# State-space products on whole operands: states copied by eight groups, tables reordered, a block's 48 small matmuls in one bunch

## The chip, the core and the metric

One core of one Trainium2 chip runs the whole program. The metric is device time in microseconds (us) of one execution. The core's engines named here are PE (TensorE: matmuls, and PEld, its weight loads), DVE (VectorE), ACT (ScalarE), POOL (GpSimd) and SP (SyncE, which issues most of the DMAs). Each has its own instruction order and they meet through semaphores.

## The reference, cut to what matters

The model is a first block (attention, mLSTM, mixture of experts) and a second block of two layers; everything here happens in the last layer, `s5_branch`, with one sequence of 256 positions and 128 groups of 16 features with 64 complex states each:

```python
u, z, xq = split_cols(h @ w_in, [SEQ_WIDTH, MIX_WIDTH, XA_WIDTH])      # 2048, 3072, 1024
y = s5_chunked(u in groups, ab, bb, c)   # x_t = ab x_{t-1} + bb u_t ;  y_t = re(c x_t)
y = jax.nn.gelu(y + d * u)
y = y * jax.nn.sigmoid(y @ w_glu + b_glu)
xa = memory_attention(xq, mem_n, w_kv)
x = x + (jnp.concatenate([y, xa], axis=-1) * jax.nn.silu(z)) @ w_out
```

## The kernel before

All weights are fp32. Each is split into a high and a low fp32r part, ACT making the high one (`whi`, L267) and DVE the low one (`wlo`, L268), and a product is three matmuls (`mm3`). A dense product `dense_t` is 48 matmuls of 128x256 on PE; after every 12 of them it lets another generator advance, so that other work is interleaved in PE's order. Every matmul is issued at L280, so the rows are told apart by tile: `ps` is a dense product, `st` a state-space product, `at` the attention, `acc` the output projection.

The state-space part splits the 256 positions into 64 chunks of 4. The 128 groups are worked on in eight blocks `jb`, each of 8 columns j and two halves x of 64 partitions. One state-space product is 64x64 on 64 partitions in fp32 and shows as two matmul rows on PE.

The layer goes through these stages:

1. **Inputs and states.** The input projections `su` give u, which goes through memory (`ud`, written by ACT's queue, L1719) and comes back as `U[jb]` (L1679). `states(jb)` multiplies U by the table `tab1` (tile `tab`, two products per j and x, real and imaginary states) and by `tab3` (tile `wu`, the product inside the chunk). It yields after every second j, and so a block's 48 products lie in PE's order in four passes between the dense products of `su` and `sx`. DVE and ACT then copy the states of every chunk to `Xs` (L1694, L1692), and DVE adds d·u to U (L1696, L1697).
2. **Scan.** `scanned(half)` is the recurrence over chunks in `Xs`, on DVE (L1638 to L1641, four operations a step, 21 steps a half). Half 0 can start after block 3, half 1 after block 7. `scan(n)` puts n steps into the order at fixed places of the stages around it.
3. **Memory attention** (`at`), then twelve `z_block`s (dense products of `sz`, each closed by a multiply on DVE, L1614), with scan steps between them.
4. **Output stage.** For each jb: the table `tab2` (L1603, two buffers, each freed by the product two blocks before) times `Xs` gives `st`; DVE adds U (L1747), ACT makes the Gelu (L1748) and issues a write to memory (`yd`, L1749), SP issues two reads back (`yy`, L1754, four buffers), ACT and DVE split each `yy` (tiles `y`, `U`), POOL multiplies it into `zs` (L1759). Beside this PE runs the output projection of the attention features f = 16 to 23 (`acc`, 24 matmuls each; its operands `gyh` and `gyl` are split from `xa` by ACT and DVE).
5. **Gated output.** For f = 0 to 15 a dense product with `sglu` on all split y (`ps`, 48 matmuls) and then 24 `acc` matmuls, to the end.

Operands are read as they lie: in L1745 the weights are `w[x, j, i::2]` (every second element) and the moving states `Xs[x, i, :, 8 * jb + j]` (every 64th element); in L1688 `wu[x, j]` is every eighth element, while `tab1`'s parts and U lie side by side.

No engine's order is written out by hand for the change: the order follows from the code, buffer waits and a scheduler.

Of the kernel before, what the change touches and what calls it, by code (L numbers as in the profile page):

```python
# [15 lines left out]
AF = mybir.ActivationFunctionType  # L16
# [191 lines left out]
class Kern:  # L208
# [1115 lines left out]
    def s5_out(self, P, jb):  # L1324

        nc, e = self.nc, self.nc.gpsimd
        raw = self.t(P, [128, 2, 8, 16], "s_raw", bufs=2)
        e.dma_start(raw, self.io["sbc"][jb][:, 2:4])
        t2 = self.t(P, [128, 8, 64, 2], "s_t2")
        tmp = self.t(P, [128, 8, 16], "s_tmp")  # L1330
        A = [self.s5ab[:, i, 8 * jb:8 * jb + 8, None].to_broadcast([128, 8, 16]) for i in range(2)]
        e.tensor_scalar(raw[:, 1], raw[:, 1], -1.0, None, op0=OP.mult)
        y = (raw[:, 0], raw[:, 1])
        for k in range(4):
            o = tuple(t2[:, :, 16 * k:16 * k + 16, i] for i in range(2))
            e.tensor_mul(o[0], y[0], A[0])
            e.tensor_mul(tmp, y[1], A[1])
            e.tensor_add(o[0], o[0], tmp)
            e.tensor_mul(o[1], y[1], A[0])
            e.tensor_mul(tmp, y[0], A[1])  # L1340
            e.tensor_sub(o[1], o[1], tmp)
            y = o
        e.dma_start(self.tab2[jb], t2.rearrange("p j s i -> p j (s i)"))

    def s5_steps(self, G, P):

# [241 lines left out]
    def s5(self, out):  # L1588
        nc, io, tc = self.nc, self.io, self.tc
        x3 = self.xT  # L1590
        self.psum_banks(ps=2, st=3, at=3)
        with ExitStack() as S:
            P = S.enter_context(tc.tile_pool(name="s", bufs=1))
            zs = self.t(P, [128, 16, T], "zs")
            xa = self.t(P, [128, 8, T], "xa")

            Xs = self.t(P, [128, 2, 64, 64], "Xs")
            U = []
            halves = [slice(0, 64), slice(64, 128)]

            def table(jb, tab):
                w = self.t(P, [128, 8, 128], "tab", bufs=2)
                nc.sync.dma_start(w, tab[jb].rearrange("p j s -> p j s"))  # L1603
                return w

            with ExitStack() as S2:
# [36 lines left out]
                def scanned(half):  # L1643

                    gs = slice(32 * half, 32 * half + 32)
                    Xb = Xs.rearrange("p i (b s) g -> p i b s g", b=8)[..., gs]
                    for n in range(1, 8):
                        onto(Xb[:, :, :, n], Xb[:, :, :, n - 1], 0, gs, [128, 2, 8, 32])
                        yield
                    for b in range(1, 8):  # L1650
                        onto(Xb[:, :, b, 7:8], Xb[:, :, b - 1, 7:8], 7, gs, [128, 2, 1, 32])
                        yield
                    for b in range(1, 8):
                        onto(Xb[:, :, b, 0:7], Xb[:, :, b - 1, 7:8], slice(0, 7), gs, [128, 2, 7, 32])
                        yield
# [3 lines left out]
                def scan(n):  # L1659
                    for _ in range(n):  # L1660
                        next(steps, None)


                with tc.tile_pool(name="su", bufs=1) as S1:
                    with tc.issue_after(self.mark.ins):
                        d = self.t(S1, [128, 64], "sd")
                        nc.sync.dma_start(d, io["sd"])
                        nc.gpsimd.memset(Xs[:, :, 0], 0.0)
                        self.s5_steps(P, S1)

                    def inputs(jb):
                        return table(jb, self.tab1.rearrange("b p j i s -> b p j (i s)")).rearrange("p j (i s) -> p j i s", i=2)

                    def states(jb, w):
                        wu = self.t(S1, [128, 4, 128], "wu", bufs=2)
                        nc.sync.dma_start(wu, self.tab3[jb])
                        wu = wu.rearrange("p k (h j) -> p j (k h)", j=8)
                        U.append(self.t(P, [128, 8, 64], "U", bufs=8))
                        nc.sync.dma_start(U[jb].rearrange("p j c -> p (j c)"), self.ud[jb])  # L1679
                        ps = [self.psum("st") for _ in range(3)]  # L1680
                        pj = [p.rearrange("p (j c) -> p j c", j=8) for p in ps]
                        for j in range(8):
                            for i in range(3):
                                for x in halves:
                                    self.mm(pj[i][x, j], wu[x, j] if i == 2 else w[x, j, i], U[jb][x, j], True, True)
                            if j % 2:
                                yield
                        for i in range(2):  # L1688
                            src = ps[i].rearrange("p (j c) -> p c j", j=8)[:, 0:63]
                            dst = Xs[:, i, 1:64, 8 * jb:8 * jb + 8]  # L1690
                            if i:
                                nc.scalar.activation(dst, src, AF.Copy)  # L1692
                            else:
                                nc.vector.tensor_copy(dst, src)  # L1694
                        t = self.t(W, [128, 8, 64], "zt")
                        nc.vector.tensor_mul(t, U[jb], d[:, 8 * jb:8 * jb + 8, None].to_broadcast([128, 8, 64]))  # L1696
                        nc.vector.tensor_add(U[jb], t, pj[2])  # L1697

                    def all_states():
                        with tc.issue_after(self.mark.ins):  # L1700
                            w = inputs(0)
                        yield
                        for jb in range(8):
                            with tc.issue_after(self.mark.ins):
                                now, w = w, inputs(jb + 1) if jb < 7 else None
                                yield from states(jb, now)
                            if jb >= 4:
                                scan(SCAN_EARLY)

                    st = all_states()  # L1710
                    next(st)
                    for n in range(4):
                        for b in (n, n + 4):
                            ps = self.dense_t(io["su"][b], h, st if 2 * n + b // 4 >= 3 else iter(())) if b else self.su0
                            u = self.t(W, [128, 2, T], "zt")
                            nc.vector.tensor_mul(u, ps, bc(r, 2))
                            for a in range(2):
                                dst = self.ud[2 * n + a].rearrange("(q s h) (j c) -> q (h j) s c", q=2, s=4, j=8)
                                nc.scalar.dma_start(dst[b // 4], u[:, a].rearrange("p (s c) -> p s c", s=4))  # L1719
                    for b in range(4):  # L1720
                        ps = self.dense_t(io["sx"][b], h, st)
                        nc.vector.tensor_mul(xa[:, 2 * b:2 * b + 2], ps, bc(r, 2))
                    for _ in st:
                        pass
# [4 lines left out]
                for b in (8, 9, 10, 11, 0, 1, 2, 3, 4, 5, 6, 7):  # L1729
                    if b == 6:  # L1730
                        scan(64)
                    z_block(b)
                    scan(SCAN_LATER)

            self.psum_banks(acc=4, ps=2, st=2)
            Y = S.enter_context(tc.tile_pool(name="sg", bufs=1))
# [1 line left out]
            ys = [[None] * 16, [None] * 16]  # L1738
            for jb in range(8):
                w = table(jb, self.tab2)  # L1740
                p = self.psum("st")
                for j in range(8):
                    for i in range(2):
                        for x in halves:
                            self.mm(p[x, 64 * j:64 * j + 64], w[x, j, i::2], Xs[x, i, :, 8 * jb + j], i == 0, i == 1)  # L1745
                y = U[jb].rearrange("p j c -> p (j c)")
                nc.vector.tensor_add(y, p, y)  # L1747
                nc.scalar.activation(y, y, AF.Gelu_apprx_tanh)  # L1748
                nc.scalar.dma_start(self.yd[jb], y)  # L1749
                yv = self.yd[jb].rearrange("(q s h) (j c) -> q (h j) s c", q=2, s=4, j=8)  # L1750
                for par in range(2):
                    f = 8 * par + jb
                    u = self.t(W, [128, T], "yy", bufs=4)
                    nc.sync.dma_start(u.rearrange("p (s c) -> p s c", s=4), yv[par])  # L1754
                    y2 = self.t(P, [128, 2, T], "U", F32R, bufs=8) if par else self.t(Y, [128, 2, T], "y%d" % jb, F32R)
                    for n in range(2):
                        ys[n][f] = y2[:, n]
                    self.split(u, ys[0][f], ys[1][f])
                    nc.gpsimd.tensor_mul(zs[:, f], zs[:, f], u)  # L1759
# [82 lines left out]
```

## Time and profile before

| what | value |
|---|---|
| median of 3 runs | 1498.87 us (1495.82 to 1501.35) |
| the profiled execution's own time | 1499.36 us |
| its span, first to last instruction | 1497.3 us |
| PE busy | 1337.9 us, 89% |
| PEld busy | 1065.1 us, 71% |
| DVE busy | 761.6 us, 51% |
| ACT busy | 549.8 us, 37% |
| POOL busy | 323.3 us, 22% |
| mean granted clock of PE | 0.93 |

The shares are averages over the whole program, and the last layer is only its last 425 us or so. What a stage can gain has to be read from that stage's windows and chain. The profiled execution is 0.5 us above the median. Records of PE start where a matmul starts and their ends are modelled, so that the distance of two starts says what one cost.

### The profile page before, as it was taken

What the parts mean: (1) busy time and instruction counts of PE and PEld (TensorE: products, weight loads), DVE (VectorE), ACT (ScalarE), POOL (GpSimd) and SP (SyncE); (2) the same over time, 40 slices, a digit from 0 to 9 for tenths busy, and PEclk for the clock granted to TensorE, in tenths of its full rate; (3) what the DMA queues carried; (4) which work ended last, traced back from release to release, by engine and by line L of the source; (5) the groups of instructions that cost most, each with busy time, mean ns of one, the idle gap of its engine ahead of it and who ended that gap; (6) DMA issues with size and microseconds to landing.
All of it is one profiled execution on the core that took longest, in us unless ns stands there. A gap on an engine that the chain in (4) does not pass through costs nothing. (4 is left out here: it accounts for less than half of the span.)

```text
span 1497.3 us, 25797 instructions
## 1 busy us (share of the span) xinstructions
PE 1337.9 (89%) x10632; PEld 1065.1 (71%) x10632; DVE 761.6 (51%) x1498; ACT 549.8 (37%) x859; POOL 323.3 (22%) x450
## 2 busy tenths in 40 slices
PE   5999998987887888686679999999999999999997
PEld 2777796553454555341159989999888988999997
DVE  2766454812233321010047686588846899665553
ACT  3754553321211122110034435644522355444443
POOL 0031121412223231200008887111400000030001
PEclk8899999998988999896689999999999999999998
DMA  9776764999999999999994525889766534675540
GB/s 364 277 268 250 268 246 174 379 400 420 420 408 415 420 408 420 420 421 374 421 370 156 204 92 178 259 251 320 265 203 204 170 138 147 213 205 189 178 141 29
DMA packets 87626, 414.86 MB, mean 277 GB/s; under 512 B 26432, under 2 KB 28016, under 8 KB 43472
## 3 DMA queue, kind: packets, MB, share of 16 engines
q1 hardware_dynamic: 66768, 381.85, 66.9%
q0 software_dynamic: 8016, 22.13, 4.7%
q10 hardware_dynamic: 12720, 9.18, 1.9%
q8 instruction: 86, 1.41, 0.4%
q14 instruction: 36, 0.29, 0.1%
HBM read 392.90 MB, written 20.22 MB: 276 GB/s over the span
## 5 line engine op out<-in xcount | busy, mean ns | idle before, releaser
L267 ACT ACTIVATE whi<-w 128x1024 fp32r<-128x1024 f32 x252 | 263.7, 1056 | 329.8 <-PE ps L280 249.9
L268 DVE TENSOR_TENSOR wlo<-w,whi 128x1024 fp32r<-128x1024 f32 x222 | 273.4, 1240 | 145.2 <-ACT whi L267 144.6
L280 PE MATMUL ps<-hh,whi 128*128 128x256 f32 x928 | 272.8, 294 | 11.2 <-DVE zt L1614 5.0
L280 PE MATMUL ps<-hh,wlo 128*128 128x256 f32 x928 | 266.9, 288 | 2.0 <-DVE wlo L268 1.8
L280 PE MATMUL ps<-hl,whi 128*128 128x256 f32 x928 | 267.8, 289 | 0.9 <-DVE hl L1579 0.7
L280 PEld LDWEIGHTS ps<-hh,whi 128*128 128x128 f32 x928 | 179.0, 193 | 19.5 <-issue 9.1
L280 PEld LDWEIGHTS ps<-hh,wlo 128*128 128x128 f32 x928 | 178.8, 193 | 4.5 <-DVE wlo L268 2.6
L280 PEld LDWEIGHTS ps<-hl,whi 128*128 128x128 f32 x928 | 179.0, 193 | 2.0 <-DVE hl L1579 0.7
L280 PE MATMUL A<-w,xg 128*32 128x512 f32 x984 | 139.6, 667 | 33.8 <-DMA w<-in_w 32.9
L280 PE MATMUL acc<-gyl,whi 128*128 128x256 f32 x384 | 109.1, 284 | 0.6 <-DVE gyl L268 0.6
L280 PE MATMUL acc<-gyh,wlo 128*128 128x256 f32 x384 | 109.1, 284 | 0.0
L280 PE MATMUL acc<-gyh,whi 128*128 128x256 f32 x384 | 108.2, 282 | 0.0
L268 POOL TENSOR_TENSOR wlo<-w,whi 128x1024 fp32r<-128x1024 f32 x30 | 70.6, 2368 | 167.1 <-ACT whi L267 166.9
L934 DVE SCALAR_TENSOR_TENSOR xT<-m,mod,xT 128x256 f32<-128x256 f32 x64 | 27.8, 480 | 142.7 <-PE m L280 142.7
L280 PEld LDWEIGHTS A<-w,xg 128*32 128x32 f32 x984 | 23.8, 114 | 102.3 <-DMA w<-in_w 73.2
L280 PE MATMUL A<-w,gT 128*32 128x512 f32 x512 | 75.0, 687 | 24.1 <-DMA w<-in_w 16.5
L960 DVE TENSOR_TENSOR g<-g,A 128x512 f32<-128x512 f32 x8 | 5.5, 687 | 134.3 <-PE A L280 134.3
L280 PEld LDWEIGHTS acc<-gyl,whi 128*128 128x128 f32 x384 | 72.7, 189 | 1.5 <-DVE gyl L268 0.8
L280 PEld LDWEIGHTS acc<-gyh,whi 128*128 128x128 f32 x384 | 73.2, 191 | 0.2 <-issue 0.2
L280 PEld LDWEIGHTS acc<-gyh,wlo 128*128 128x128 f32 x384 | 72.9, 190 | 0.2 <-issue 0.2
L1759 POOL TENSOR_TENSOR zs<-zs,yy 128x256 f32<-128x256 f32 x16 | 14.7, 935 | 236.9 <-DMA yy<-yd 236.1
L280 PE MATMUL ps<-wlo,hh 128*128 128x256 f32 x192 | 56.1, 292 | 3.4 <-DVE wlo L268 3.4
(585 smaller groups left out, 2766.8 us busy)
## 6 DMA issues: line engine op xcount, KB each, us to landing
w<-in_w SPq DMA_DIRECT2D x187, 1024.0 KB, 11.5
w<-in_wada SPq DMA_DIRECT2D x24, 1024.0 KB, 7.3
w<-in_wo SPq DMA_DIRECT2D x24, 1024.0 KB, 5.3
w<-in_sglu SPq DMA_DIRECT2D x16, 1024.0 KB, 4.9
w<-in_gz SPq DMA_DIRECT2D x12, 1024.0 KB, 6.9
w<-in_sz SPq DMA_DIRECT2D x12, 1024.0 KB, 4.8
w<-in_win SPq DMA_DIRECT2D x10, 1024.0 KB, 7.1
w<-in_xk SPq DMA_DIRECT2D x8, 1024.0 KB, 9.7
```

Of the source, the lines that this page charges most:

```text
L267: self.nc.scalar.activation(hi, src, AF.Copy)
L268: (eng or self.nc.vector).tensor_sub(lo, src, hi.bitcast(F32))
L280: self.nc.tensor.matmul(ps, l, r, start=start, stop=stop, **kw)
L934: self.nc.vector.scalar_tensor_tensor(self.xT[:, f], pc[:, T * c:T * c + T], self.m(5)[:, f:f + 1], self.xT[:, f], op0=OP.mult, op1=OP.add)
L960: nc.vector.tensor_mul(g1, g1, p3)
L1759: nc.gpsimd.tensor_mul(zs[:, f], zs[:, f], u)
```

## The change

- `tab2` is stored with the real parts of a j ahead of the imaginary ones (the POOL code that builds it writes them so), and so a weight operand is 64 elements side by side.
- `Xs` becomes two tiles, one for each half of the scan. A new helper `by_group` has ACT copy a block of 8 columns to `Xg`, with the 64 chunks of one column side by side (128x1024, eight copies: one in the attention stage, seven in the output stage, two buffers). The output products read `Xg`.
- `tab3` is loaded to a free part of `zs`, and ACT copies it (128x512, eight copies) to `wu` so that a weight operand is side by side.
- A block's 48 products in `states` are issued in one bunch. The four yields come behind them.

```diff
-        t2 = self.t(P, [128, 8, 64, 2], "s_t2")
+        t2 = self.t(P, [128, 8, 2, 64], "s_t2")
...
-            Xs = self.t(P, [128, 2, 64, 64], "Xs")
+            Xs = [self.t(P, [128, 2, 64, 32], "Xs%d" % n) for n in range(2)]
...
+                def by_group(pool, jb):
+                    Xg.append(self.t(pool, [128, 2, 8, 64], "Xg", bufs=1 if jb == 0 else 2))
+                    nc.scalar.activation(Xg[jb], Xs[jb // 4][:, :, :, 8 * (jb % 4):8 * (jb % 4) + 8].rearrange("p i c j -> p i j c"),
+                                         AF.Copy)
...
-                        wu = self.t(S1, [128, 4, 128], "wu", bufs=2)
-                        nc.sync.dma_start(wu, self.tab3[jb])
-                        wu = wu.rearrange("p k (h j) -> p j (k h)", j=8)
+                        raw = zs[:, 2 * (jb % 4):2 * (jb % 4) + 2].rearrange("p f t -> p (f t)")
+                        nc.sync.dma_start(raw, self.tab3[jb].rearrange("p k c -> p (k c)"))
+                        wu = self.t(S1, [128, 8, 64], "wu", bufs=2)
+                        nc.scalar.activation(wu.rearrange("p j (k h) -> p j k h", k=4),
+                                             raw.rearrange("p (k h j) -> p j k h", k=4, j=8), AF.Copy)
...
                                     self.mm(pj[i][x, j], wu[x, j] if i == 2 else w[x, j, i], U[jb][x, j], True, True)
-                            if j % 2:
-                                yield
...
                         nc.vector.tensor_add(U[jb], t, pj[2])
+                        for _ in range(4):
+                            yield
...
+                by_group(P, 0)
...
                 w = table(jb, self.tab2)
+                if jb < 7:
+                    by_group(Y, jb + 1)
...
-                            self.mm(p[x, 64 * j:64 * j + 64], w[x, j, i::2], Xs[x, i, :, 8 * jb + j], i == 0, i == 1)
+                            self.mm(p[x, 64 * j:64 * j + 64], w[x, j, 64 * i:64 * i + 64], Xg[jb][x, i, j], i == 0, i == 1)
```

On PE, in the input and state stage, a piece of the difference between the two orders (`x4` is four products in a row: the real and the imaginary part of one j on both halves of the partitions):

```order
 L280 MATMUL st<-U,tab 64x64 x4
 L280 MATMUL st<-U,wu 64x64 x2
-L280 MATMUL ps<-hl,whi 128x256
-L280 MATMUL ps<-hh,wlo 128x256
-L280 MATMUL ps<-hh,whi 128x256
-L280 MATMUL ps<-hl,whi 128x256
-L280 MATMUL ps<-hh,wlo 128x256
 L280 MATMUL st<-U,tab 64x64 x4
 L280 MATMUL st<-U,wu 64x64 x2
```

The dense rows between two j are gone from here and stand behind the bunch: before there are 43 separate stretches of `st` rows among the `ps` rows of this stage, now 8 stretches of 48 products. The products (384) and the `ps` rows between the first of them and the first `at` (413) are as many as before.

SP's DMA issues in the same stage, around the loads of blocks 2 and 3, before:

```order
L262 DMA w<-in_sx 128x2048
L1679 DMA U<-ud 128x512 x2
L1603 DMA tab<-tab_84 128x1024
L1676 DMA wu<-tab_86 128x512
L262 DMA w<-in_sx 128x2048
```

and in the changed kernel (L1690 is U's load, L1685 the load of `tab3` to `zs`):

```order
L262 DMA w<-in_sx 128x2048
L1603 DMA tab<-tab_84 128x1024
L1690 DMA U<-ud 128x512 x2
L1685 DMA zs<-tab_86 128x512
L262 DMA w<-in_sx 128x2048
```

The loads U(2) and U(3) moved behind the load of `tab` for block 3, which waits until the bunch of block 1 has let go of its buffer.

ACT in the output stage, before (with the tiles' numbers; `U_11117` is U of block 7, its Gelu is L1748 and its write L1749):

```order
L267 ACTIVATE gyh_12831<-xa_9999 128x256
L267 ACTIVATE whi_12903<-w_12901 128x1024
L1748 ACTIVATE U_11117<-U_11117 128x512
L267 ACTIVATE y5_12585<-yy_12583 128x256
L1749 DMA yd_87<-U_11117 128x512
L267 ACTIVATE U_12591<-yy_12589 128x256
```

and in the changed kernel (`U_11127` is U of block 7, Gelu L1762, write L1763):

```order
L267 ACTIVATE gyh_12857<-xa_9999 128x256
L267 ACTIVATE U_12563<-yy_12561 128x256
L267 ACTIVATE whi_12895<-w_12861 128x1024
L267 ACTIVATE whi_12929<-w_12927 128x1024
L267 ACTIVATE y5_12609<-yy_12607 128x256
L1762 ACTIVATE U_11127<-U_11127 128x512
L267 ACTIVATE U_12615<-yy_12613 128x256
L1763 DMA yd_87<-U_11127 128x512
```

The Gelu of block 7 moved behind the split `y5`, which waits for block 5's read back from memory. In the same stage ACT has the seven copies `Xg` and one load of an activation table more than before; ahead of the Gelu of block 0 stand the copies `Xg` of blocks 1 and 2, the `gyh` of f = 16 and 17 and a table load.

SP's issues in the output stage of the changed kernel (`yy` is L1768):

```order
L262 DMA w<-in_wo 128x2048
L1603 DMA tab<-tab_85 128x1024 x2
L1768 DMA yy<-yd 128x4x64 x2
L1603 DMA tab<-tab_85 128x1024
L1768 DMA yy<-yd 128x4x64 x2
L1603 DMA tab<-tab_85 128x1024 x2
L1768 DMA yy<-yd 128x4x64 x4
L1603 DMA tab<-tab_85 128x1024
```

The table of block 4 is behind the first two `yy`, those of blocks 5 and 6 behind the next two, and that of block 7 behind the `yy` of blocks 2 and 3; before, the tables of blocks 3 and 4 stood together ahead of the first `yy` and the fifth's behind four of them.

## Rows read from the trace of the kernel before

**Rows 1.** Windows of the last layer, one line each. The columns are start:end, length, then for PE, PEld, DVE, ACT and POOL the busy us and the number of instructions, the granted clock, the share of DMA engines busy and GB/s. The first two make up the stage of inputs and states, cut where the scan begins; then attention and z-blocks; the output stage; the gated output.

```profile
1099.78:1145.31 45.53, 45.53 (x582) 40.95 (x582) 19.65 (x25) 10.82 (x12) 0.00 (x0) 1.00 0.62 193
1145.31:1190.00 44.69, 44.69 (x573) 40.72 (x571) 36.78 (x68) 10.56 (x12) 0.00 (x0) 1.00 0.56 184
1190.00:1290.48 100.48, 91.30 (x687) 87.43 (x685) 97.71 (x199) 55.01 (x71) 0.00 (x0) 0.98 0.44 151
1290.48:1344.81 54.33, 53.74 (x706) 51.86 (x707) 30.29 (x42) 24.71 (x45) 14.68 (x16) 0.97 0.73 228
1344.81:1497.30 152.49, 143.73 (x1188) 143.35 (x1187) 72.98 (x90) 64.65 (x88) 7.25 (x8) 0.96 0.38 132
```

**Rows 2.** The chain of work that ended last, input and state stage: start, us, engine, tile, line, matmul rows.

```profile
1101.73 1.09 PE st L280 x24
1102.82 1.62 PE ps L280 x12
...
1187.71 5.89 PE ps L280 x48
1193.60 0.86 PE at L280 x4
```

**Rows 3.** Timeline of PE at two places of that stage: start, us with the modelled end, engine, line, tile and operands, rows.

```profile
1107.07 0.45 PE L280 MATMUL st<-U,tab 64*64 64x64 f32 x8
1107.35 0.40 PE L280 MATMUL st<-U,wu 64*64 64x64 f32 x4
1107.59 0.40 PE L280 MATMUL st<-U,tab 64*64 64x64 f32 x8
1107.82 0.40 PE L280 MATMUL st<-U,wu 64*64 64x64 f32 x4
...
1181.17 0.68 PE L280 MATMUL st<-U,tab 64*64 64x64 f32 x16
1181.78 0.39 PE L280 MATMUL ps<-hl,whi 128*128 128x256 f32 x1
```

**Rows 4.** Tile `st`: matmuls by operand, with the duration of one in ns (minimum/median/maximum) and the first and last start.

```profile
L280 PE MATMUL st<-U,tab x512: 218/218/267, 1099.8 to 1187.3; 64*64 64x64 f32 x171
L280 PE MATMUL st<-Xs,tab x512: 283/285/309, 1290.5 to 1329.6; 64*64 64x64 f32 x171
L280 PE MATMUL st<-U,wu x256: 275/280/330, 1100.0 to 1187.4; 64*64 64x64 f32 x128
```

**Rows 5.** Timeline of DVE at the first scan step and at the last z-block, and between them one weight split from the chain of work that ended last.

```profile
1145.31 0.68 DVE L1638 TENSOR_TENSOR zs<-Xs,pw 128x512 f32<-128x512 f32 x1
...
1271.05 1.14 DVE wlo L268
...
1289.75 0.68 DVE L1614 TENSOR_TENSOR zt<-ps,r 128x512 f32<-128x512 f32 x1
```

**Rows 6.** The chain of work that ended last, output stage and the first gated product (columns as in rows 2; a block's 32 products are 64 rows, and a few records are missing, so that x125 stands for the 128 rows of blocks 0 and 1).

```profile
1290.48 7.33 PE st L280 x125
1299.20 3.72 PE st L280 x64
...
1334.30 2.72 DMA yy<-yd
...
1337.91 0.96 DVE gyl L268
1338.91 5.89 PE acc L280 x47
1344.81 11.52 PE ps L280 x96
```

**Rows 7.** ACT's groups of instructions in the output stage (busy us, mean ns of one, idle before them and what ended it), and from tile `Xs` its copy of the states from PSUM, which writes every 64th element (ns minimum/median/maximum).

```profile
L267 ACT ACTIVATE whi<-w 128x1024 fp32r<-128x1024 f32 x8 | 8.4, 1053 | 6.2 <-PE acc L280 6.2
L1748 ACT ACTIVATE U<-U 128x512 f32<-128x512 f32 x8 | 5.1, 633 | 15.6 <-DVE U L1747 15.6
L267 ACT ACTIVATE y<-yy 128x256 fp32r<-128x256 f32 x8 | 3.3, 407 | 3.4 <-DMA yy<-yd 2.9 <-ACT U L1748 0.4
L1748 ACT ACT_TABLE_LOAD x1 | 1.3, 1283 | 0.0
...
L1692 ACT ACTIVATE Xs<-st x8: 576/592/593, 1109.1 to 1187.5; 128x504 f32<-128x504 f32 x8
```

**Rows 8.** DMAs, us from issue to landing (minimum/median/maximum): tiles `ud`, `U`, `yd`, `yy`, and `tab` in the output stage, in this order; one issue on SP's queue in the output stage; then POOL's multiply of `yy`, from the page's costliest groups.

```profile
DMA to landing us min/median/max: 2.0/4.9/8.3
DMA to landing us min/median/max: 2.3/4.3/6.2
DMA to landing us min/median/max: 2.2/4.2/6.0
DMA to landing us min/median/max: 2.2/4.1/5.6
DMA to landing us min/median/max: 4.1/4.9/5.7
...
1309.35 0.33 SPq L1603 DMA_DIRECT2D tab<-tab  x1
...
L1759 POOL TENSOR_TENSOR zs<-zs,yy 128x256 f32<-128x256 f32 x16 | 14.7, 935 | 236.9 <-DMA yy<-yd 236.1
```

**Rows 9.** A window of dense matmuls of 128x256 a little before the state stage (columns as in rows 1).

```profile
1076.00:1079.30 3.30, 3.30 (x16) 3.30 (x17) 2.38 (x4) 1.58 (x3) 3.22 (x5) 0.50 0.78 276
```

More of the change, by code (lines that the diff above doesn't have):

```diff
@@ L1334, in s5_out @@
         for k in range(4):
-            o = tuple(t2[:, :, 16 * k:16 * k + 16, i] for i in range(2))
+            o = tuple(t2[:, :, i, 16 * k:16 * k + 16] for i in range(2))
             e.tensor_mul(o[0], y[0], A[0])
@@ L1342, in s5_out @@
             y = o
-        e.dma_start(self.tab2[jb], t2.rearrange("p j s i -> p j (s i)"))
+        e.dma_start(self.tab2[jb], t2.rearrange("p j i s -> p j (i s)"))
     def s5_steps(self, G, P):
@@ L1645, in scanned @@
                     gs = slice(32 * half, 32 * half + 32)
-                    Xb = Xs.rearrange("p i (b s) g -> p i b s g", b=8)[..., gs]
+                    Xb = Xs[half].rearrange("p i (b s) g -> p i b s g", b=8)
                     for n in range(1, 8):
@@ L1661, in scan @@
                         next(steps, None)
+                Xg = []
+                def by_group(pool, jb):
+                    Xg.append(self.t(pool, [128, 2, 8, 64], "Xg", bufs=1 if jb == 0 else 2))
+                    nc.scalar.activation(Xg[jb], Xs[jb // 4][:, :, :, 8 * (jb % 4):8 * (jb % 4) + 8].rearrange("p i c j -> p i j c"),
+                                         AF.Copy)
                 with tc.tile_pool(name="su", bufs=1) as S1:
@@ L1667, in s5 @@
                         nc.sync.dma_start(d, io["sd"])
-                        nc.gpsimd.memset(Xs[:, :, 0], 0.0)
+                        for x in Xs:
+                            nc.gpsimd.memset(x[:, :, 0], 0.0)
                         self.s5_steps(P, S1)
@@ L1685, in states @@
                                     self.mm(pj[i][x, j], wu[x, j] if i == 2 else w[x, j, i], U[jb][x, j], True, True)
-                            if j % 2:
-                                yield
                         for i in range(2):
                             src = ps[i].rearrange("p (j c) -> p c j", j=8)[:, 0:63]
-                            dst = Xs[:, i, 1:64, 8 * jb:8 * jb + 8]
+                            dst = Xs[jb // 4][:, i, 1:64, 8 * (jb % 4):8 * (jb % 4) + 8]
                             if i:
```

## Prediction
> **What bounds the layer now.** I read the windows first, then the chain, then the timelines of the places where the chain changes engine. PE is busy for all of the input and state stage (45.53 of 45.53 and 44.69 of 44.69 us) [rows 1], and the chain is PE alone there, dense rows and state-space rows in turn [rows 2]. From the first scan step at 1145.31 on a second line runs beside it: DVE is busy for 36.78 + 97.71 = 134.5 of the 145.2 us up to 1290.48 [rows 1, 5]. The 10.7 us that it idles lie mostly ahead of 1190 (7.9), where it waits for PE; after that it idles 2.8. PE idles 9.2 us in that second stretch. So from 1190 to the first output product DVE is the fuller one, and what the end of that stretch hangs on is when the scan can begin. The last z-block's multiply starts at 1289.75 [rows 5] and the first output product at 1290.48 [rows 6]. In the output stage PE is busy for 53.74 of 54.33 us [rows 1], with a last wait on the reads `yy` and the split of f = 23 near its end [rows 6]. The gated output (152.5 us) is not touched; it starts when f = 23 is done.
>
> **States stage.** Eight rows on side-by-side operands take 0.235 us on average (1107.07 to 1107.35 with the switch, 1107.59 to 1107.82), 29.4 ns a row; four rows on `wu` 0.24, 59 ns [rows 3]. Sixteen rows of the first kind between dense ones take 0.61 instead of 0.47, and a whole pass of 16 + 8 rows 1.09 instead of 0.94 [rows 2, 3]; the 12 dense rows behind it take 1.62 instead of 12 x 0.12 = 1.44 (5.89 for 48 gives 0.12) [rows 2]. So changing between dense and small products costs about 0.15 + 0.17 = 0.32 us a pass. The stage from the first bunch to the first `at` is then
>
> 413 x 0.12 + 512 x 0.0294 + 256 x 0.0588 + 43 x 0.32 = 49.6 + 15.1 + 15.1 + 13.8 = 93.5,
>
> against 93.8 in the trace (1099.78 to 1193.60) [rows 1, 2]. With the change: 413 x 0.12 + 768 x 0.0294 + 8 x 0.32 = 74.7, that is 18.8 less: 7.5 from `wu` and 11.2 from 35 passes that are gone.
>
> Two things are put against it. The load U(2) now stands on SP behind the table of block 3, which waits for bunch 1. Bunches follow each other at 7.8 to 8.9 us, and the way of u to U is a multiply (0.7), the write `ud` (4.9) and the read (4.3) by the medians [rows 8], 9.9 us of the 10 or so that lie between; I take 1.2 us of wait for bunch 2, with 0 and 5 (the slow ends 8.3 and 6.2) as bounds. And ACT makes eight copies to `wu`: its nearest row is the copy of 504 elements at 0.59 [rows 7]; ACT is busy for 21 of the stage's 90 us [rows 1], so they are hidden, unless one stands right ahead of a `whi`, at 0.6 each.
>
> **Scan start to first output product.** Bunch 3 ends near 1129.6 by the same count (1099.78, 1107.8, 1116.7 + 1.2, 1126.8 for the starts), and with the copy and the add of about 0.7 each on DVE the scan begins at 1131.3, 14.0 earlier. Up to the last z-block DVE has the same work as now and, by its order, three `wlo` (1.14 each [rows 5]) and a `zt` more in this stretch: 134.5 + 4.0. What is left of idle time is the open number. Now it is 10.7, most of it waiting for PE, and PE runs ahead by 19 now; I take the 2.8 that it has after 1190 [rows 1]. First output product: 1131.3 + 138.5 + 2.8 = 1272.6, **17.9 earlier**. PE's own line gives the same: first `at` at 1174.5 + 1.2, and the 96.9 us from there to 1290.48 unchanged make 1272.6. Bounds: no idle time 20.7; all 10.7 us of it kept, 10.0; with slow U loads as well, 8.5.
>
> **Output stage.** A block's 64 rows take 3.7 us now (57 to 58 ns a row) [rows 6]; side by side on both operands I take the 29.4 of the states stage, 1.9 us a block. No row shows these two operands packed; the bounds are 29.4 and 57. PE's work falls from 29.4 + 192 x 0.12 + about 1.4 to 15 + 23 + 2 = 40.5. But each block hangs on a chain through memory, and there the change of order counts. With medians from [rows 7, 8], in us behind the first product:
>
> - ACT: silu, `gyh`, Xg(1), Xg(2), `gyh`, a table load of 1.28, then Gelu 0; Xg copies at 1.05 like the 128x1024 `whi` (at most 1.2, twice the strided copy). Block 1 ends at 3.9, `yd`(0) is issued at 6.4 and lands at 10.7.
> - SP: the reads `yy`(0) then go, and tab(4) behind them, with 0.33 an issue: it lands at 16.6. PE has by then done blocks 0 to 3 and 39 `acc`, at 12.7, and waits 3.9. Block 4 ends at 18.5, which frees tab(6)'s buffer: it lands at 23.8, block 6 ends at 25.7.
> - tab(7) stands behind `yy`(2) and `yy`(3), whose writes are issued at 18.5 and 18.9: it lands at 29.2, block 7 ends at 31.1 (39.4 now).
> - `yd`(5) is issued at 30.3, lands at 34.6, `yy`(5) at 38.8. The Gelu of block 7 stands behind the split `y5`, and so ends at 39.8 though its product was done at 31.1. Its write lands at 44.5, `yy`(7) at 48.8, the split to 49.2, then `gyh` and `gyl` of f = 23 to 52.2, and 24 `acc` at 0.12 (5.89 for 47 [rows 6]): 55.
>
> So the stage keeps about its length (54.3 now), and PE's 13 us become idle time in it. In gaps of this size the clock may fall: dense rows are 0.206 apart at a granted clock of 0.50 (16 in 3.30 [rows 9]) against 0.12. I add 1.6 for this, with 0 and 18 (all 192 `acc`) as bounds: 56.6, **2.3 more** than now. Bounds of the chain: by the shortest landings PE's work is the limit, about 45 (9 less); by the longest (yd 6.0, yy 5.6 over four round trips) 68 (14 more).
>
> POOL builds `tab2` in another element order with the same operations, and its wait for `yy` is what its multiply shows [rows 8]; it is not on the chain. The yields at the end of `states` add nothing by themselves.
>
> **Sum.** 1499.4 − 17.9 + 2.3 = 1483.8 against the profiled execution's 1499.36, which is 0.5 above the median: **1484**.
>
> **Rivals.**
> - A (0.52): as worked out, 1484, own range 1479 to 1488.
> - B (0.17): the output stage is bounded by PE, not by the round trips, because landings are short or ACT's order costs nothing. For it: PE is busy for 99% of the stage now [rows 1], so the trace shows no round trip that PE had to wait for but the last. Against it: `y5` ahead of the Gelu of block 7. 1499.4 − 18 − 9 = 1472.
> - C (0.17): the gain of the states stage is lost in part before the output stage: DVE keeps its 10.7 us of idle time, or U comes late at blocks 2 and 4. For it: the scan steps stand at fixed places among dense rows, and U's way takes nearly all the time that there is. 1499.4 − 9 + 0 to 2 = 1490 to 1492.
> - D, on the other side (0.06): PE's gaps in the output stage put the granted clock at 0.50 for nearly all of it. 192 `acc` cost 0.09 more each, 17, and the products are back at 58 ns a row, 14 more: 40.5 + 31 and half of the 15 us of gaps make a stage of about 79 instead of 54, and 1499.4 − 18 + 25 = 1506. It decides from where some two thirds of the stage lie at half clock. Against it: the stage shows 0.97, and 0.98 stands in the stretch where PE idles 9 us [rows 1].
> - E (0.08): the products don't get faster, since a fixed weight load sets their pace; then only the passes (11.2) and nothing from `wu`, and the first output product comes about 11 earlier: 1488. Against it: rows at 29.4 ns on `tab` stand beside rows at 59 on `wu`, with the same 64x64 on 64 partitions, and the medians of one matmul differ likewise (218 and 280) [rows 3, 4].
>
> Beside E: the Trainium skill, page "TensorE: Matmul & The Clock Gate", section "LDWEIGHTS (loading the stationary operand)", has a weight load last as many cycles as it has columns, at 1.2 per ns, however many rows. By it 64 columns are an estimated 53 ns, the stride of the operand would not matter, and the new layouts would gain nothing. The trace doesn't agree for these operands: sixteen rows in 0.61 us, switch included, are 38 ns a row [rows 3].
>
> **How the numbers follow.** A, B, C and E are faster than 1491.4 but for about half of C's and a little of A's chance; 0.5% (7.5 us) is about what a measurement of this kernel can tell from no change. Faster 0.82, the same 0.12, slower 0.06 (D and long landings). The range has to reach from B to C's end to leave out no more than 2 in 10: 1471 to 1494.
>
> **What would show it.** After: 8 stretches of `st` rows of about 2.8 us (96 x 29.4 ns) in the states stage, first `at` 94 − 19 = 75 us behind the first of them; rows on `wu` with the median of those on `tab`; scan start some 14 earlier relative to the first bunch; first output product 17 to 19 earlier; in the output stage PE idle 13 to 16 us, ended by `tab`, `yy` and DVE; block 7's Gelu waiting behind `y5`; no more than 57 us from first product to the first gated row. The prediction is wrong if DVE's idle time from scan to z-block is near 10 (then C), if the output stage is down to 45 (B), if its clock is below 0.7 (D), or if rows on `wu` and `Xg` still come 57 ns apart (E).

## The result and the profile after

The changed kernel takes 1480.33 us (1478.85 to 1481.63) against 1500.11 us in the same comparison: a ratio of 0.9863, interval 0.9842 to 0.9884, some 20 us. Forecast were 1484 and, from the profiled execution of the kernel before, a gain of 15.6.

The windows of the layer in the changed kernel, columns as in [rows 1]: first bunch to scan start, to first attention matmul, to first output product, to the first gated row, to the end.

```profile
1102.44:1132.38 29.94, 29.77 (x530) 29.06 (x531) 16.56 (x21) 12.35 (x14) 0.00 (x0) 1.00 0.73 237
1132.38:1176.70 44.32, 44.32 (x654) 43.51 (x653) 44.18 (x88) 16.78 (x18) 0.00 (x0) 1.00 0.62 214
1176.70:1276.59 99.89, 90.09 (x659) 85.20 (x657) 95.30 (x184) 58.74 (x73) 0.00 (x0) 0.97 0.44 153
1276.59:1325.87 49.28, 42.29 (x706) 40.62 (x707) 28.01 (x40) 38.11 (x53) 14.09 (x16) 0.97 0.77 235
1325.87:1478.30 152.43, 142.93 (x1189) 142.55 (x1187) 73.00 (x90) 64.52 (x88) 7.23 (x8) 0.97 0.38 133
```

Against [rows 1], span to span (1478.3 and 1497.3): the first bunch starts 2.7 later (1102.44, before 1099.78), the scan 15.6 earlier after it (29.9, before 45.5), scan to first product takes 1.0 less (144.2, before 145.2), the output stage 5.1 less (49.3, before 54.3), the gated output is the same. Sum −19.0. Between scan start and first attention matmul DVE is now busy for 44.18 of 44.32 us; in the whole stretch to the first product it idles 4.7 us instead of 10.7. The stretch is only 1.0 shorter all the same, because DVE has 5.0 us more work in it (139.5, before 134.5).

The chain in the state stage of the changed kernel, columns as in [rows 2]:

```profile
1102.44 3.02 PE st L280 x96
1105.46 5.06 PE ps L280 x41
1110.52 2.97 PE st L280 x96
...
1113.80 5.58 DMA U<-ud
...
1119.52 3.02 PE st L280 x96
1122.54 5.89 PE ps L280 x48
```

A bunch is 96 rows in 3.0 us. The read of U(2), behind the table of block 3, lands just in time: PE's timeline shows 0.17 us of idle time ahead of bunch 2. The products and the new copies, by tile (ns minimum/median/maximum, first and last start):

```profile
L280 PE MATMUL st<-U,tab x512: 218/218/267, 1102.4 to 1166.4; 64*64 64x64 f32 x171
L280 PE MATMUL st<-U,wu x256: 218/218/218, 1102.7 to 1166.5; 64*64 64x64 f32 x128
L280 PE MATMUL st<-Xg,tab x512: 218/218/313, 1276.6 to 1307.9; 64*64 64x64 f32 x171
```

```profile
L1687 ACT ACTIVATE wu<-zs x8: 1125/1205/1235, 1078.3 to 1149.5; 128x512 f32<-128x512 f32 x8
...
L1668 ACT ACTIVATE Xg<-Xs x8: 1972/2036/2143, 1199.5 to 1301.3; 128x1024 f32<-128x1024 f32 x8
```

All three kinds of product have the duration that only `tab` had in [rows 4]. The copies took twice what the forecast had for them.

ACT in the attention stage of the changed kernel (timeline; in brackets the idle time before, and what ended it):

```profile
1196.50 0.60 ACT L1168 ACTIVATE xa<-at 128x512 f32<-128x512 f32 x1 [1.14 <-PE at L280]
1199.50 2.14 ACT L1668 ACTIVATE Xg<-Xs 128x1024 f32<-128x1024 f32 x1 [2.40 <-DVE Xs L1641]
1201.66 1.28 ACT L1158 ACT_TABLE_LOAD   x1
1202.96 0.47 ACT L1158 ACTIVATE xp<-at,xmx 128x256 f32<-128x256 f32 x1
```

The scheduler put Xg(0) here: ACT stops for 2.4 us until half 0 is scanned, copies for 2.1, and an exponential of the attention waits behind it.

PE's starts after idle time in the output stage of the changed kernel (timeline):

```profile
1279.60 2.08 PE L280 MATMUL st<-Xg,tab 64*64 64x64 f32 x64 [0.94 <-ACT Xg L1668]
1285.57 3.95 PE L280 MATMUL st<-Xg,tab 64*64 64x64 f32 x128 [0.22 <-DMA tab<-tab]
1293.18 3.37 PE L280 MATMUL st<-Xg,tab 64*64 64x64 f32 x64 [2.28 <-DVE U L1761]
1305.99 2.08 PE L280 MATMUL st<-Xg,tab 64*64 64x64 f32 x64 [1.01 <-DMA tab<-tab]
1315.63 0.39 PE L280 MATMUL acc<-gyl,whi 128*128 128x256 f32 x1 [1.49 <-DVE gyl L268]
1322.86 0.38 PE L280 MATMUL acc<-gyl,whi 128*128 128x256 f32 x1 [1.07 <-DVE gyl L268]
```

The landings of `yd` and of `yy` there, as in [rows 8]:

```profile
DMA to landing us min/median/max: 2.0/3.6/5.6
DMA to landing us min/median/max: 2.2/3.6/4.3
```

ACT around the Gelu of block 7 and the last `y` (timeline), and ahead of it the write of block 5, DVE's add for block 7, and POOL's multiply that waits for the same read as `y5`:

```profile
1304.50 0.38 ACTq L1763 DMA_DIRECT2D yd<-U  x1
1308.78 0.68 DVE L1761 TENSOR_TENSOR U<-st,U 128x512 f32<-128x512 f32 x1
1309.68 1.51 POOL L1773 TENSOR_TENSOR zs<-zs,yy 128x256 f32<-128x256 f32 x1 [1.43 <-DMA yy<-yd]
...
1309.63 0.42 ACT L267 ACTIVATE y<-yy 128x256 fp32r<-128x256 f32 x1
1309.96 0.62 ACT L1762 ACTIVATE U<-U 128x512 f32<-128x512 f32 x1
...
1319.38 0.42 ACT L267 ACTIVATE y<-yy 128x256 fp32r<-128x256 f32 x1 [4.07 <-DMA yy<-yd]
```

The places of the forecast are there: block 4 late, block 7 waiting for its table, the Gelu of block 7 right behind `y5`, the last reads close to the end. But they cost less, and the idle time of PE is 7.0 us and not 13 to 16. Block 4 started 16.6 behind the first product, as forecast, though what ended its wait last was an add on DVE and not its table. And the read that `y5` needs had landed by 1309.68, hardly later than DVE was done with block 7 (1309.46): standing behind `y5` kept the Gelu of block 7 waiting for about half a microsecond.

### The profile page after: what moved, and what is told of

Read it like the earlier page. It is cut to its first block, busy times and chain, and to the rows that moved or that the text cites. A ratio compares the mean times of both kernels' runs of the same rounds, so it can differ in the third digit from the quotient of the medians.

```text
span 1478.3 us, 25813 instructions
## 1 busy us (share of the span) xinstructions
PE 1317.6 (89%) x10632; PEld 1044.7 (71%) x10632; DVE 762.4 (52%) x1498; ACT 576.4 (39%) x878; POOL 323.2 (22%) x451
## 5 line engine op out<-in xcount | busy, mean ns | idle before, releaser
L280 PE MATMUL ps<-hh,whi 128*128 128x256 f32 x928 | 271.3, 292 | 10.7 <-DVE zt L1614 4.0
L280 PE MATMUL A<-w,xg 128*32 128x512 f32 x984 | 143.9, 685 | 32.1 <-DMA w<-in_w 31.3
```

What stands on the lines that cost most here:

```text
L280: self.nc.tensor.matmul(ps, l, r, start=start, stop=stop, **kw)
```

## The experiments

Each kernel ran beside the kernel before, whose medians were 1499.8 to 1501.0. The stages are those of one profiled execution, in us (the output stage is counted to the start of the first gated row on PE's timeline, 0.1 to 0.2 earlier than in the windows above). That execution's own time stands beside the median, since it can lie far from it: 10 us above in e10, 7 above in e7, 5.5 below in e3. The ratio is given by its interval:

| kernel | first bunch to scan | scan to first product | DVE busy in that | output stage | profiled execution | median | ratio to before |
|---|---|---|---|---|---|---|---|
| before | 45.5 | 145.2 | 134.5 | 54.2 | 1499.4 | | |
| changed | 29.9 | 144.2 | 139.5 | 49.1 | 1480.2 | 1480.3 | 0.9842 to 0.9884 |
| e1_passes | 43.3 | 143.5 | 136.4 | 53.4 | 1495.1 | 1492.1 | 0.9930 to 0.9959 |
| e2_wu | 33.4 | 150.2 | 140.1 | 52.3 | 1493.5 | 1491.3 | 0.9911 to 0.9956 |
| e3_out | 29.9 | 139.9 | 138.6 | 54.5 | 1477.1 | 1482.6 | 0.9866 to 0.9902 |
| e4_tab | 30.6 | 139.6 | 138.5 | 55.8 | 1480.9 | 1480.4 | 0.9855 to 0.9899 |
| e5_xg | 30.3 | 144.5 | 139.3 | 49.3 | 1480.0 | 1482.8 | 0.9842 to 0.9904 |
| e6_pool0 | 30.2 | 140.8 | 139.6 | 51.8 | 1483.2 | 1479.4 | 0.9817 to 0.9868 |
| e7_spread | 29.8 | 158.1 | 150.1 | 50.8 | 1499.8 | 1492.9 | 0.9908 to 0.9957 |
| e8_pool0_spread | 30.0 | 160.3 | 151.4 | 52.0 | 1501.4 | 1499.9 | 0.9973 to 1.0006 |
| e9_pool023 | 29.9 | 140.8 | 139.6 | 51.2 | 1477.4 | 1477.4 | 0.9827 to 0.9872 |
| e10_grouped | 30.4 | 178.7 | 178.3 | 55.9 | 1530.1 | 1519.8 | 1.0092 to 1.0140 |
| e11_tab3 | 29.7 | 142.9 | 140.1 | 52.0 | 1483.4 | 1479.2 | 0.9827 to 0.9876 |
| e12_bunch | 33.4 | 143.2 | 139.1 | 55.2 | 1486.6 | 1487.5 | 0.9882 to 0.9948 |

**The parts of the state stage.** e1 puts the yields back:

```diff
+                            if j % 2:
+                                yield
...
-                        for _ in range(4):
-                            yield
```

> The changed kernel with one part undone: the yields stand inside the 48 products again, so a block lies in four or more passes between dense rows. Some 35 more passes at 0.32 us are 11.2 us of PE in the states stage, of which about 5 lie ahead of the scan's start (blocks 0 to 3: some 20 passes instead of 4). Theory A (from the scan's start on DVE sets the end): the scan and the first output product come about 5 us later and so does the end: 1485 against 1480. Rival (PE sets the end all the way): the whole 11 us, 1491. Rival (the passes cost nothing, the gain is the layouts' alone): 1480.

e2 loads `wu` as before; e12 is the kernel before with the bunch alone (the edit of e1 the other way round).

```diff
-                        raw = zs[:, 2 * (jb % 4):2 * (jb % 4) + 2].rearrange("p f t -> p (f t)")
-                        nc.sync.dma_start(raw, self.tab3[jb].rearrange("p k c -> p (k c)"))
-                        wu = self.t(S1, [128, 8, 64], "wu", bufs=2)
-                        nc.scalar.activation(wu.rearrange("p j (k h) -> p j k h", k=4),
-                                             raw.rearrange("p (k h j) -> p j k h", k=4, j=8), AF.Copy)
+                        wu = self.t(S1, [128, 4, 128], "wu", bufs=2)
+                        nc.sync.dma_start(wu, self.tab3[jb])
+                        wu = wu.rearrange("p k (h j) -> p j (k h)", j=8)
```

> The changed kernel with wu loaded as before and read at every eighth element, without ACT's eight copies. 256 rows at 59 instead of 29.4 ns are 7.5 us of PE, 3.8 of them ahead of the scan's start. Theory A (DVE sets the end from the scan's start): 3.8 later, 1484. Rival (PE all the way): 7.5 later, 1488. Rival (the copies on ACT and the later load cost as much as they give): 1480.

> The kernel before with one part of the change alone: a block's 48 products in one bunch, the yields behind it. Undoing this part cost 13.2 us between the first bunch and the first attention matmul (87.5 against 74.3), undoing wu alone 7.4 (81.7). If the parts add, this kernel has 93.7 - 13 = 80 to 82 us there, the 95 to 97 of the kernels without copies Xg up to the first output product, an output stage as before (54 to 56), and takes 1486 to 1489 against 1500. Rival (bunching pays only with packed wu, since a bunch with strided rows keeps DVE and ACT waiting longer): 1493 or more.

From first bunch to first attention matmul it is 93.7 before, 87.5 in e1, 81.7 in e2 and in e12, 74.3 in the changed kernel. So the bunch is worth 12 to 13 us of PE (forecast 11.2) and packed `wu` 6 to 7.4 (7.5), and they add. e12 came out as expected (81.7 there, 94.9 on to the first product, 55.2 in the output stage, 1487.5). Three windows: e1 up to the scan, then e2 and e12 from the scan's start to the first attention matmul.

```profile
1100.54:1143.82 43.28, 43.28 (x584) 38.49 (x584) 19.36 (x25) 15.09 (x16) 0.00 (x0) 0.96 0.66 197
1136.39:1184.68 48.29, 48.29 (x656) 47.47 (x654) 45.18 (x88) 14.05 (x15) 0.00 (x0) 1.00 0.63 209
1133.51:1181.79 48.28, 48.28 (x655) 47.46 (x654) 45.17 (x88) 14.05 (x15) 0.00 (x0) 1.00 0.62 210
```

In time, e1 met the rival's number, but not by the rival's reason. The scan starts 13.3 later, not 5, and from there it takes 143.5, about as in the changed kernel: e1's expectation counted the passes and forgot that with the yields inside a block its last products stand behind more dense rows. By the records, the window to the scan's start holds 190 dense rows in e1 and 146 in the changed kernel, 5.3 us at 0.12; 23 stretches of small rows instead of 4 are 6.1 at 0.32 each; and the granted clock is 0.96 instead of 1.00. e2's expectation failed. It moves the scan by the 3.5 that were expected, but then loses another 4.0 up to the first attention matmul (48.3, changed kernel 44.3): PE is busy there all the time and DVE is not, so the strided rows of blocks 4 to 7 count in full, and e12 shows the same 48.3. Up to the attention it is PE that sets the pace as soon as it has more to do. The rest of the 13.3 us by which e2's profiled execution is longer lies in the attention and z-blocks (2.1) and in the output stage (3.2), where its granted clock is 0.93 instead of 0.97. What set that clock is not shown.

**Which stretch DVE sets.** The window from scan start to first product in the changed kernel:

```profile
1132.38:1276.59 144.21, 134.41 (x1311) 128.71 (x1309) 139.49 (x270) 75.52 (x91) 0.00 (x0) 0.98 0.50 172
```

The same in e4, in e6, and in e7:

```profile
1130.97:1270.53 139.56, 132.52 (x1310) 127.58 (x1308) 138.47 (x270) 73.75 (x90) 0.00 (x0) 0.99 0.51 173
```
```profile
1135.99:1276.78 140.79, 132.23 (x1310) 127.29 (x1309) 139.64 (x270) 73.89 (x90) 4.23 (x1) 0.99 0.51 172
```
```profile
1136.48:1294.62 158.14, 136.25 (x1310) 130.76 (x1309) 150.07 (x258) 75.07 (x91) 32.61 (x12) 0.95 0.46 157
```

e4 has no copies Xg, and e6 has Xg(0) on POOL:

```diff
-                    nc.scalar.activation(Xg[jb], Xs[jb // 4][:, :, :, 8 * (jb % 4):8 * (jb % 4) + 8].rearrange("p i c j -> p i j c"),
-                                         AF.Copy)
+                    block = Xs[jb // 4][:, :, :, 8 * (jb % 4):8 * (jb % 4) + 8].rearrange("p i c j -> p i j c")
+                    if jb == 0:
+                        nc.gpsimd.tensor_copy(Xg[jb], block)
+                    else:
+                        nc.scalar.activation(Xg[jb], block, AF.Copy)
```

> The changed kernel with the copy Xg(0) made by POOL instead of ACT. In the changed kernel ACT stands still for 2.4 us in the attention stage until the scan of half 0 is done and then copies for 2.1, with an exponential and high weight parts behind it; from first attention matmul to first output product it takes 99.9 us there and 95.2 and 95.6 in the two runs without any Xg. Theory (this copy holds up ACT's queue): that stretch goes to 95 to 96, and the time to 1476. Rival (the stretch differs by the clock of that execution, which fell to half for a while): 97 to 100, time 1480. Rival (POOL's copy slows DVE): 100 or more.

With ACT's stop gone, the stretch is DVE's work and 1.1 us (139.56 and 138.47; 140.79 and 139.64). So DVE does set it in these kernels, and the copy on ACT cost 3.4 to 4.7. In e12, which has no copies either but strided `wu`, it takes 143.2, because of the part in which PE is the fuller one. From the attention to the first product e6 took 96.5 (95 to 96 expected), but it gave 2.7 back in the output stage of its execution, at a granted clock of 0.93 instead of 0.97, and its time is not told apart from the changed kernel's.

From the attention to the last z-block, e7 gives every second low weight part to POOL (12 of them); e8 is e6 and e7 together.

```diff
+                self.spread = 1
                 self.mem_attention(V, xa, kv1, xa, lambda: scan(SCAN_HEAD))
...
+                self.spread = 0
                 by_group(P, 0)
```

> The changed kernel with half of the low weight parts (wlo) from the attention stage to the last z-block made by POOL, which has nothing to do there, instead of DVE: 12 or 13 of 27 at 1.2 us are some 15 us less for DVE, at 2.4 us each on POOL. Prediction's theory (DVE sets the end from the scan's start to the first output product): that stretch (144.2 us) gets shorter by what PE leaves, 6 to 10 us, 1470 to 1474. Rival (PE, the attention's chain and ACT's order set it): 0 to 3 us, 1477 to 1480. Rival (POOL's low parts come too late for PE, or its work slows DVE's): longer, 1481 to 1486.

> Both of the two before at once: Xg(0) and half of the low weight parts on POOL. If the two waits are apart, the gains add: 1468 to 1473. If both come out of the same idle time of PE in the attention stage (about 8 us with the lower clock behind it), it is no better than the better one by more than 1 us; if POOL is then late, it is worse than either.

e7 was 12 us slower than the changed kernel, and not faster. DVE had 12 instructions less and was busy for 10.6 us more. Its timeline in e7, and then POOL's:

```profile
1219.87 0.67 DVE L1641 TENSOR_TENSOR Xs<-zs 128x512 f32<-128x512 f32 x1
1220.53 3.35 DVE L268 TENSOR_TENSOR wlo<-w,whi 128x1024 fp32r<-128x1024 f32 x1
1223.80 0.68 DVE L1638 TENSOR_TENSOR zs<-Xs,pw 128x512 f32<-128x512 f32 x1
```
```profile
1219.97 2.83 POOL L268 TENSOR_TENSOR wlo<-w,whi 128x1024 fp32r<-128x1024 f32 x1 [8.85 <-ACT whi L267]
```

A low part of 1.2 us takes 3.35 on DVE: POOL's own runs to 1222.80, and 1.1 after that DVE's is done, as if it had stood still until POOL was finished. The Trainium skill, page "SBUF — State Buffer", section "Who interferes with whom", says that a DVE instruction with two SBUF inputs contends with a GpSimd instruction that reads SBUF; the trace agrees. Most of DVE's added time is in the scan. Its first operation on 128x448, from DVE's groups in this stretch of e7 and then of the changed kernel:

```profile
L1638 DVE TENSOR_TENSOR zs<-Xs,pw 128x448 f32<-128x448 f32 x14 | 14.6, 1045 | 0.1
L1638 DVE TENSOR_TENSOR zs<-Xs,pw 128x448 f32<-128x448 f32 x14 | 8.8, 625 | 0.1
```

Moving work to an idle POOL lost time here, and e8 lost all 20 us. Why e8 is 7 slower than e7 by the median is open; their profiled executions differ by 1.6.

**The operands of the output stage.** e3 undoes both, e4 keeps tab2's new order and drops Xg, e5 keeps Xg and drops the order. Of the product's call in the changed kernel (first line) and in e3, e4 and e5 (in this order), the two operands:

```diff
-    w[x, j, 64 * i:64 * i + 64], Xg[jb][x, i, j]
...
+    w[x, j, i::2], Xs[jb // 4][x, i, :, 8 * (jb % 4) + j]
...
+    w[x, j, 64 * i:64 * i + 64], Xs[jb // 4][x, i, :, 8 * (jb % 4) + j]
...
+    w[x, j, i::2], Xg[jb][x, i, j]
```

> The changed kernel with the output products as before: tab2's parts interleaved, the moving operand read from Xs at every 32nd element, no copies Xg on ACT. Theory (the layouts gave the output stage its 5 us): the stage from first product to first gated row goes from 49 back to 54, 1485 in all. Rival (the stage is bound by its round trips through memory, and 5 us came from shorter landings in that one execution): stage 49 to 51, time as the changed kernel or up to 2 less because ACT has no copies.

> The changed kernel with tab2's parts apart, but the moving operand read from Xs at every 32nd element and no copies Xg. It tells which operand's stride slows a row. If the moving operand's: rows of 57 ns and a stage as long as with both undone (54). If the weights': rows of 29 ns without 16 us of copies on ACT, stage 46 to 49, and the time 0 to 3 below the changed kernel.

> The changed kernel with tab2's parts interleaved again (weights read at every second element), the copies Xg kept. With tab2's parts apart and no Xg a row took 57 ns, so the moving operand's stride alone sets the pace there. If every second element costs nothing: rows of 29 ns as in the changed kernel, output stage 49, 1480. If it costs too: rows between 29 and 57, stage 50 to 54, 1481 to 1485.

Tile `st` in e4, and then in e5:

```profile
L280 PE MATMUL st<-Xs,tab x512: 283/285/302, 1270.5 to 1307.9; 64*64 64x64 f32 x171
```
```profile
L280 PE MATMUL st<-Xg,tab x512: 219/221/367, 1276.4 to 1307.6; 64*64 64x64 f32 x171
```

The moving operand's stride (32 elements) alone makes the slow row; weights at every second element cost nothing to speak of (221, with 219 for the products on U in the same execution), at every eighth they did (280, [rows 4]). The Trainium skill, page "SBUF — State Buffer" (the note on cachelines), puts the free stride of fp32 at 4 elements; 2, 8 and 32 fall on the sides that it says. So the table's new order bought nothing. Xg made the output stage 5.2 to 6.7 us shorter in these four executions (49.1 and 49.3 against 54.5 and 55.8), and its first copy took 3.4 to 4.7 of that away in the attention stage. But the other kernels with Xg took 50.8 to 53.4 in the output stage, and e10 below, whose products read whole operands without any copy, 55.9: what the fast rows are worth to this stage is not settled. In time, e3 and e4 are not told apart from the changed kernel, so the bunch and `wu` account for 17 to 19 of the 20 us.

**Other places for the copy.** e9 has Xg(0), (2) and (3) on POOL; e11 makes Xg(0) in the output stage and uses the room for a third table buffer; e10 lays `Xs` out by column (`[128, 2, 32, 64]`), so that no copy is needed and the scan reads and writes every 64th element. Of their edits, one line of e9 (against e6), two of e11 and one of e10:

```diff
-                    if jb == 0:
+                    if jb in (0, 2, 3):
...
-                by_group(P, 0)
...
-                w = self.t(P, [128, 8, 128], "tab", bufs=2)
+                w = self.t(P, [128, 8, 128], "tab", bufs=3)
...
-                    Xb = Xs[half].rearrange("p i (b s) g -> p i b s g", b=8)
+                    Xb = Xs[half].rearrange("p i g (b s) -> p i b s g", b=8)
```

> The changed kernel with the copies Xg of blocks 0, 2 and 3 on POOL (4.2 us each there, against 2.0 on ACT) and the other five on ACT. In the output stage ACT is busy for all of the first 10 us, with two copies, 4 us, ahead of the first Gelu, and the first write is issued 7.1 us behind the first product. Theory (ACT's queue and the round trips behind it bound the output stage): the first write comes 2 us earlier, the stage is 47 to 49 instead of 49 to 53, attention to first product 96, in all 1476. Rival (PE or the last reads bound it): as with Xg(0) alone on POOL, 1479. Rival (POOL's copies are late for blocks 2 and 3): 1482 or more.

> The changed kernel with the copy Xg(0) moved behind the last z-block to the output stage (which frees its buffer) and a third buffer for the tables. Two waits are taken away: ACT's stop in the attention stage, and the tables of blocks 4 to 7 waiting for the product two blocks before. One is added: the first product waits 2 us for its copy. Theory (round trips and table loads bound the output stage): attention to first product 96 to 98, output stage 47 to 49, 1476 to 1478. Rival (tables are not what it waits for): output stage 51 to 53 by the first copy, 1480 to 1482.

> The changed kernel without copies Xg, with Xs itself laid out by column (the 64 chunks of a column side by side), so that the output products read it whole and the scan on DVE works on every 64th element. The state copies from PSUM become plain. If DVE pays nothing for the stride (its rows stay at 0.6 to 0.69 us): attention to first product 95, output stage 47 to 49, 1473 to 1477. If DVE pays like ACT does for Xg (twice): 0.6 us more for most of 168 scan operations, some 60 to 90 us more between scan start and first product, 1540 to 1570.

e9 is the fastest of all by median, 1477.4, and gains in the stretch expected (140.8); its output stage was 51.2, not 47 to 49, and its first write was issued 6.7 behind the first product instead of 7.1, not 2 us earlier, because two table loads of ACT now stand ahead of the first Gelu. In e11 the rival came true (52.0): its products waited 6.0 us for copies, and it lost there more than it won in the attention. Neither interval stands apart from the changed kernel's. e10 shows what the copies save, in DVE's groups there:

```profile
L1638 DVE TENSOR_TENSOR zs<-Xs,pw 128x512 f32<-128x512 f32 x14 | 14.9, 1064 | 0.0
```

Such an operation had 0.68 [rows 5]: 56% more for the stride, 39 us more of DVE's work than in the changed kernel (178.3 of 178.7 us), and with DVE full the stretch is 34 longer, most of the loss. DVE pays less than the doubling expected, and the time was 1520, not 1540 or more. Its output stage missed the 47 to 49 expected too: 55.9, with 6.2 of wait for tables and a granted clock of 0.91.

## Why the prediction was right, point by point

- **Rows and passes.** The pace held for `wu`: inside a bunch 12 rows start every 0.35 us, 29.2 ns a row (96 rows take 2.97 to 3.02), and the stage took 74.3 from first bunch to first attention matmul (75.9 forecast, with 1.2 of wait for U that did not come). Rival E fell: with whole operands the rows on `wu` and `Xg` have the 218 of `tab`, so no fixed weight load holds them at 57. The weight loads' own records (PEld) are 135 ns for whole operands and 213 for strided `wu` in the kernel before; they overlap each other, so the pace of the rows does not tell what one load takes.
- **Scan start.** 15.6 earlier (14.0 forecast). U(2) was only just in time (0.17 of wait, 1.2 forecast), which put bunch 3 some 1.1 earlier; the other 0.5 lies between the end of bunch 3 and the scan.
- **DVE sets the rest.** Right: work 139.5 (138.5 forecast). Idle time 4.7, not 2.8. The step that failed is the price and place of ACT's copies: "Xg copies at 1.05 like the 128x1024 `whi` (at most 1.2...)" and 0.6 for `wu`. They took 2.04 and 1.2. They read every 32nd and every 8th element, and the rows that they were priced on read side by side; no run makes the same copy on ACT without the stride, so that the stride is the reason is argued and not shown. And the copy in the attention stage had no term at all: it cost 3.4 to 4.7 us. By e4 and e6, without it the stretch would have been 140 to 141, the 141.3 forecast.
- **Output stage.** 2.3 longer was forecast, 5.1 shorter it was: the wrong direction, and here the mechanism held only in part. Up to the last product the chain was as worked out: block 4 began at 16.6 (forecast 16.6) and block 7 ended 31.5 behind the first product (31.1). The step that failed is the wait of block 7's Gelu for `y5`. The forecast has it end at 39.8, because `yd`(5) is issued at 30.3 and its read lands at 38.8. It ended at 34.0: the write was issued at 27.9, and write and read took 5.2 together instead of 8.5. From there to the last `y` it took 9.2, about as forecast (9.4), so these 5.8 us go through to the end; with the 1.6 for the clock, which was not lost (0.97, as before), they make up the difference between 56.6 and 49.3.
- **The output stage in the other kernels.** It was not one lucky execution: in the six other kernels with this order on ACT (e1, e2, e5 to e8) that Gelu waited 0.9 to 2.2 us, and the median landings were 3.6 to 3.8 for `yd` and 3.3 to 3.8 for `yy`, where the forecast took 4.2 and 4.1 from the kernel before. Why they are shorter there is open. These kernels took 49.3 to 53.4, none the 56.6. Why one execution took 49 and another 53 is open as well: the two at 49 show a granted clock of 0.97 in the stage, and those of 50.8 to 53.4 one of 0.91 to 0.93 and an end of that Gelu about 2 to 3 us later; but e9, at 1.00, took 51.2, waiting for tables.
- **First bunch.** It started 2.7 later. In the other kernels it started between 1098.4 and 1110.7. In the changed kernel the granted clock was 0.51 from 1080 to 1082, where it had been 1.00 before. That it comes from the change is not shown.
- **Sum.** 15.6 forecast and 19 to 20 measured. The states stage carried it, and there the mechanism was right. That the total came within 4 us is in part luck: an unseen loss of about 4 (the copy on ACT), a first bunch 2.7 later, and an unseen gain of 7 in the output stage did not quite cancel. Three slips of the working change nothing in it: 0.235 for eight rows is the step without a switch and not the average of the two shown (0.255); 15 + 23 + 2 is 40 and not 40.5; and with slow U loads as well, the first product would by the stated bounds (5 of wait for U, all of DVE's idle time kept) come 6.2 earlier and not 8.5.

## What to carry over

Small fp32 products are worth laying out: a row at a wide stride of either operand (8 elements of the weights, 32 or 64 of the moving operand) ran at half pace here. Price the reordering copy on a row of the same engine that reads at the same stride. Count where the copy lands in an engine's order and what stands behind it, not only its duration. When one engine is full over a long stretch, look at what lets that stretch begin: most of this gain came from an earlier start of the scan, in good part by moving other work behind the products that it waits for. And check whether another engine is as full in a part of that stretch: where PE was, DVE's bound did not hide PE's extra work (e2, e12).

## What the runs showed of the hardware

- Reading at a stride cost PE (57 against 29.4 ns a row at 32 elements of the moving operand, e4) and DVE (1.06 us for 512 against 0.68 at 64 elements, e10) differently. ACT's copy at 32 elements took 2.04 for 1024, beside 1.05 for its `whi` that reads side by side. POOL's copies of such blocks took 4.2 in the attention stage (e6 and e9), and 2.5 and 2.1 in the output stage (e9); the reason is not shown.
- DVE and POOL, both reading two inputs, held each other up: up to 3.35 us for an operation of 1.2 on DVE, and up to 3.21 for one of 2.4 on POOL (e7).
